# The six level products of two recurrences, split into 64-column halves of the TensorE array

## The chip, the core and the metric

The kernel runs on one core of one Trainium2 chip, in one launch. The time is device microseconds of that core, from one execution to the next; three runs of the kernel before are at hand, and one further execution that was profiled. TensorE (PE) does matrix products: a weight load puts the stationary operand into its 128 x 128 array (rows: what is summed over; columns: positions of the result), and a matmul streams the moving operand through it into PSUM. PE in a profile is its matmuls, PEld its weight loads. DVE is VectorE, ACT ScalarE.

## The reference, cut to what matters

The model is one first block of two layers and one second block. Two of its mixers are gated recurrences computed in chunks of 64 tokens, four heads each. Within a chunk they need a lower triangular matrix of weighted products (HGRN2 in the first block, GLA in the second; the two differ in head width, 128 and 64):

```python
b = jnp.cumsum(gi, axis=2)                                  # log decay in a chunk of 64
diff = b[:, :, :, None, :] - b[:, :, None, :, :]
dec = jnp.exp(jnp.where(tri, diff, -jnp.inf))
att = jnp.einsum('bhtk,bhtsk,bhsk->bhts', qi, dec, ki)      # t, s in one chunk
o_intra = jnp.einsum('bhts,bhsv->bhtv', att, vi)
```

Around them stand projections from 1024 columns, attention of two kinds, a pooling mixer, two MLPs, and a mixture of 32 experts.

## The kernel before, in words

The sequence has 512 tokens and 16 leading ones. Every float32 weight is split into a high and a low part and multiplied in three products (`dense`, L289), with loads of 512 KB streamed from memory; this is most of TensorE's work.

The decay in `att` depends on both positions and on the key, so it can't be taken out of the product at once. The kernel does it by levels: for w = 1, 2, 4, 8, 16, 32 (`LEVELS`), pairs of neighbouring blocks of w positions, the second against the first, get their decay relative to the block border. `level` (L518 to L540, DVE and ACT) makes one array x for a level, in which the first blocks hold the keys and the second blocks the queries; one matmul per tile of 128 tokens (two chunks) then multiplies x with itself. In `att_level` the stationary operand is the tile's 128 positions of x, the moving one the 64 positions that `second` picks (the second block of each pair), and the result stands in a PSUM tile of 128 x 64 (L557). A `copy_predicated` on DVE (L561) then takes the entries of that level by a mask (`self.msk`) into `at` (HGRN2) or `gat` (GLA). `att_diag` (L569) makes the diagonal before.

- `hgrn_head` runs four times, once a head: rows is one slice of 128, so a level is 4 matmuls, one a tile. For levels 0 to 3 a further small matmul does the 16 leading tokens (L767, 8 moving columns; L769 reads its first 16 rows).
- `gla_heads` runs twice, for two heads each: a pair of heads shares the 128 rows, 64 each, so a level is 8 matmuls, two a tile, one on array rows 0 to 63 and one on rows 64 to 127.

All of these products are plain float32. The trace has two weight loads and two matmul records for each such matmul in the program.

The kernel is written as generators (`weave`, `WEAVES`), which interleave a head of a recurrence with projections and attention; a scheduler then fixes the order on each engine when the program is built. So a level's matmuls stand as a group on TensorE between groups of L289 and of attention (L1020, L1034, L2053, L2060, L2035).

Of the kernel before, what the change touches and what calls it, by code (L numbers as in the profile page):

```python
# [20 lines left out]
NM = 16  # L21
# [179 lines left out]
class Ker:  # L201
# [347 lines left out]
    def att_level(self, i, x, rows, off, ats):  # L549

        nc = self.nc
        w = LEVELS[i]
        pas = [self.psb() for _ in rows]
        for j in range(NT):
            for pa, r in zip(pas, rows):
                xs = x[r, off + j * 128:off + (j + 1) * 128]
                nc.tensor.matmul(pa[:, j * 64:(j + 1) * 64], xs, self.second(xs, i), start=True, stop=True)  # L557
        nb = 64 // w
        m = self.msk[:, i, :].rearrange("p (n b) -> p n b", b=w)[:, None].to_broadcast([128, 4, nb, w])
        for pa, at in zip(pas, ats):  # L560
            nc.vector.copy_predicated(self.second(at, i), m, pa[:, :256].rearrange("p (j n b) -> p j n b", j=4, b=w))  # L561
# [174 lines left out]
    def hgrn_head(self, p1, hd, st):  # L736
        nc = self.nc
        kk, b, c, q, v = (st[n] for n in ("kk", "b", "c", "q", "v"))

        ks = self.tmp()  # L740
        e3 = ks[:, NM:].rearrange("p (c n) -> p c n", n=64)
        c3 = c[:, NM:].rearrange("p (c n) -> p c n", n=64)
        b3 = b[:, NM:].rearrange("p (c n) -> p c n", n=64)
        nc.vector.tensor_add(e3, c3, b3[:, :, 63:64].to_broadcast([128, 8, 64]))
        nc.vector.tensor_scalar(ks[:, :NM], c[:, :NM], b[:, NM - 1:NM], None, op0=OP.add)
        nc.scalar.activation(ks, ks, AF.Exp)
        dec = p1.tile([128, 8], F32, name="dec", bufs=2)
        nc.scalar.activation(dec, b3[:, :, 63], AF.Exp)

        at = p1.tile([128, 4, 128], F32, name="at")  # L750
        am = p1.tile([128, NM], F32, name="am")
        al = [slice(0, 128)]
        self.att_diag(kk, q, al, NM, [at])
        pa = self.psb()
        nc.tensor.matmul(pa[:, :NM], kk[:, :128], q[:, :NM], start=True, stop=True)
        nc.vector.tensor_mul(am, pa[:, :NM], self.ident[:, :NM])
        x = self.level(0, b, c, None, q, T, NM)
        yield
        kt = p1.tile([128, 5, 128], F32, name="kt")
        self.to_tokens(ks, kt)  # L760
        for i in range(6):
            nxt = self.level(i + 1, b, c, None, q, T, NM) if i < 5 else None
            yield
            self.att_level(i, x, al, NM, [at])
            if i < 4:
                pa = self.psb()
                nc.tensor.matmul(pa[:, :8], x[:, :128], self.second(x[:, :NM], i), start=True, stop=True)  # L767
                w = LEVELS[i]
                nc.vector.copy_predicated(self.second(am[:NM], i), self.msk[:NM, i, :8].rearrange("p (n b) -> p n b", b=w),  # L769
                                          pa[:NM, :8].rearrange("p (n b) -> p n b", b=w))  # L770
            x = nxt
        qp = self.tmp()
        nc.scalar.activation(qp, b, AF.Exp)
        nc.vector.tensor_mul(qp, qp, q)
        yield

        ps = [self.psb() for _ in range(2)]
        new = [ps[ch % 2][:, ch // 2 * 128:(ch // 2 + 1) * 128] for ch in range(8)]
        nc.tensor.matmul(new[0], kt[:, 4, :], v[:, 4, :], start=True, stop=True, skip_group_check=True)
        for ch in range(1, 8):  # L780
            j, par = divmod(ch - 1, 2)
            r = slice(par * 64, par * 64 + 64)
            nc.tensor.matmul(new[ch], kt[r, j, :], v[r, j, :], start=True, stop=True, skip_group_check=True)
        sts = []
        for ch in range(8):
            s1 = p1.tile([128, 128], F32, name="st", bufs=8)
            if ch == 0:
                nc.vector.tensor_copy(s1, new[ch])
            else:
                nc.vector.scalar_tensor_tensor(s1, sts[-1], dec[:, ch - 1:ch], new[ch], op0=OP.mult, op1=OP.add)  # L790
            sts.append(s1)
            if ch % 2:
                yield
        yield
        po = self.psb()
        for ch in range(8):
            j, par = divmod(ch, 2)
            if par == 0:
                nc.tensor.matmul(po[:, j * 128:(j + 1) * 128], v[:, j, :], at[:, j, :], start=True, stop=False,
                                 skip_group_check=True)  # L800
            nc.tensor.matmul(po[:, ch * 64:(ch + 1) * 64], sts[ch], qp[:, NM + ch * 64:NM + (ch + 1) * 64], start=False,
                             stop=par == 1, skip_group_check=True)
        pom = self.psb()
        nc.tensor.matmul(pom[:, :NM], v[:, 4, :], am, start=True, stop=True)
        o = self.tmp()
        nc.scalar.copy(o[:, NM:], po)
        nc.scalar.copy(o[:, :NM], pom[:, :NM])

        sq = self.tmp()
        nc.scalar.activation(sq, o, AF.Square)  # L810
        yield
        yield
        pn = self.ones_sum([(self.ones, sq)])
        ro = self.tmp()
        self.rstd_rows(self.v2(ro), pn, 128)
        while "g" not in st:
            yield
        g = st["g"]
        nc.vector.scalar_tensor_tensor(g, o, self.vec("hgain"), g, op0=OP.mult, op1=OP.mult)
        nc.vector.tensor_mul(self.o[hd], g, ro)  # L820
        yield
# [1298 lines left out]
```

## Time and profile before

| | |
|---|---|
| time, median of 3 runs | 1751.21 us (1749.43 to 1753.71) |
| the profiled execution | 1755.02 us, span 1753.1 us |
| PE busy | 1705.3 us, 97% of the span |
| PEld busy | 1497.2 us, 85% |
| DVE busy | 1090.5 us, 62% |
| ACT busy | 861.0 us, 49% |
| matmul records of L557 | 384, from 80.2 to 268.3 us and from 1255.6 to 1369.3 us |

Busy time is the union of the instructions' durations. A matmul's record lasts longer than its place in the stream, since successive matmuls overlap; what one costs in a row of them is read from the distance of the starts, or from the chain that ended last, where pieces stand end to end.

### The profile page before, as it was taken

What the parts mean: (1) busy time and instruction counts of PE and PEld (TensorE: products, weight loads), DVE (VectorE), ACT (ScalarE), POOL (GpSimd) and SP (SyncE); (2) the same over time, 40 slices, a digit from 0 to 9 for tenths busy, and PEclk for the clock granted to TensorE, in tenths of its full rate; (3) what the DMA queues carried; (4) which work ended last, traced back from release to release, by engine and by line L of the source; (5) the groups of instructions that cost most, each with busy time, mean ns of one, the idle gap of its engine ahead of it and who ended that gap; (6) DMA issues with size and microseconds to landing.
All of it is one profiled execution on the core that took longest, in us unless ns stands there. A gap on an engine that the chain in (4) does not pass through costs nothing.

```text
span 1753.1 us, 26914 instructions
## 1 busy us (share of the span) xinstructions
PE 1705.3 (97%) x10674; PEld 1497.2 (85%) x10674; DVE 1090.5 (62%) x1885; ACT 861.0 (49%) x1419; POOL 59.1 (3%) x65
## 2 busy tenths in 40 slices
PE   8999999999999999999999999999999999999996
PEld 8999999999999999878888888767767788888884
DVE  7678675633434344553434345589857768999995
ACT  6455654432323134441314144454346359999995
POOL 0000000000000000000000000100000000101102
PEclk9999999999999999999999999999969999999998
DMA  5211113232323222133333234322201458999993
GB/s 189 72 49 49 37 37 105 86 96 85 96 86 96 86 96 74 59 96 97 96 95 92 90 96 143 114 61 72 73 13 55 172 213 299 323 341 358 354 363 89
DMA packets 72339, 223.72 MB, mean 128 GB/s; under 512 B 9464, under 2 KB 9520, under 8 KB 72208
## 3 DMA queue, kind: packets, MB, share of 16 engines
q1 hardware_dynamic: 68976, 215.70, 36.7%
q0 software_dynamic: 3232, 6.25, 1.9%
q8 instruction: 85, 1.39, 0.3%
q14 instruction: 46, 0.38, 0.1%
HBM read 213.50 MB, written 12.60 MB: 129 GB/s over the span
## 4 chain that ended last, share of the span: by engine, by line
PE 91%; DVE 5%; ACT 2%; DMA 1%; issue 1%; SPq 0%; POOL 0%; POOLq 0%; DVEq 0%
PE pm L289 32%; PE ps L289 29%; PE ps L1589 6%; PE ps L1569 3%; PE ps L266 3%; PE ps L267 2%; PE ps L268 2%; PE ps L557 2%; DVE wlo L260 1%; PE ps L2060 1%; PE ps L2035 1%; PE ps L2053 1%; PE pm L485 1%; PE ps L1192 1%; DVE acc L1835 1%
## 5 line engine op out<-in xcount | busy, mean ns | idle before, releaser
L259 ACT CAST whi<-wraw 128x1024 fp32r<-128x1024 f32 (+1 forms) x309 | 321.3, 1045 | 606.1 <-PE pm L289 293.0
L260 DVE TENSOR_TENSOR wlo<-wraw,whi 128x1024 fp32r<-128x1024 f32 (+1 forms) x309 | 373.1, 1216 | 40.9 <-ACT whi L259 30.6
L289 PE MATMUL pm<-xh,whi 128*128 128x264 f32 x976 | 202.1, 288 | 8.4 <-ACT whi L259 6.0
L289 PE MATMUL pm<-xh,wlo 128*128 128x264 f32 x976 | 200.7, 286 | 0.5 <-DVE wlo L260 0.5
L289 PE MATMUL pm<-xl,whi 128*128 128x264 f32 x976 | 200.4, 287 | 0.1
L289 PE MATMUL ps<-xh,whi 128*128 128x512 f32 x472 | 191.8, 407 | 0.0
L289 PE MATMUL ps<-xh,wlo 128*128 128x512 f32 x472 | 186.1, 395 | 0.0
L289 PE MATMUL ps<-xl,whi 128*128 128x512 f32 x472 | 185.3, 393 | 0.0
L289 PEld LDWEIGHTS pm<-xh,whi 128*128 128x128 f32 x976 | 152.7, 190 | 9.4 <-ACT whi L259 6.0
L289 PEld LDWEIGHTS pm<-xh,wlo 128*128 128x128 f32 x976 | 152.4, 189 | 0.8 <-DVE wlo L260 0.7
L289 PEld LDWEIGHTS pm<-xl,whi 128*128 128x128 f32 x976 | 152.0, 189 | 0.7 <-DVE xl L467 0.6
L289 PEld LDWEIGHTS ps<-xh,whi 128*128 128x128 f32 x472 | 89.1, 189 | 23.5 <-issue 1.8
L289 PEld LDWEIGHTS ps<-xh,wlo 128*128 128x128 f32 x472 | 89.0, 189 | 21.0
L289 PEld LDWEIGHTS ps<-xl,whi 128*128 128x128 f32 x472 | 89.2, 189 | 19.5 <-issue 0.5
L1589 PE MATMUL ps<-wlo,xg 128*128 128x512 f32 x256 | 103.8, 405 | 1.3 <-DVE wlo L260 1.2
L289 PE MATMUL pm<-ah,whi 128*128 128x264 f32 x512 | 104.1, 284 | 0.0
L289 PE MATMUL pm<-ah,wlo 128*128 128x264 f32 x512 | 104.0, 285 | 0.0
L289 PE MATMUL pm<-al,whi 128*128 128x264 f32 x512 | 103.7, 284 | 0.0
L1589 PE MATMUL ps<-whi,xg 128*128 128x512 f32 x256 | 103.6, 405 | 0.0
L289 PE MATMUL ps<-ah,whi 128*128 128x512 f32 x256 | 101.1, 395 | 0.0
L289 PE MATMUL ps<-ah,wlo 128*128 128x512 f32 x256 | 101.0, 394 | 0.0
L289 PE MATMUL ps<-al,whi 128*128 128x512 f32 x256 | 100.5, 392 | 0.0
(500 smaller groups left out, 3216.1 us busy)
## 6 DMA issues: line engine op xcount, KB each, us to landing
wraw<-in_stream_dram SPq DMA_DIRECT2D x306, 512.0 KB, 3.7
t<-in_stream_dram SPq DMA_DIRECT2D x90, 256.0 KB, 6.9
h<-in_stream_dram SPq DMA_DIRECT2D x37, 512.0 KB, 5.9
h<-in_xT_dram SPq DMA_DIRECT2D x16, 264.0 KB, 3.3
hd<-h SPq DMA_DIRECT2D x8, 256.0 KB, 2.0
h<-hd SPq DMA_DIRECT2D x8, 256.0 KB, 3.3
out_dram<-t SPq DMA_DIRECT2D x8, 256.0 KB, 2.1
gt<-rbd POOLq DMA_DIRECT2D x4, 256.0 KB, 5.7
```

The costliest lines, as they stand in the source:

```text
L259: self.nc.scalar.copy(hi, src)
L260: i = self.nc.vector.tensor_sub(lo, src, hi.bitcast(F32))
L266: nc.tensor.matmul(ps, wh, xh, start=start, stop=False)
L267: nc.tensor.matmul(ps, wh, xl, start=False, stop=False)
L268: nc.tensor.matmul(ps, wl, xh, start=False, stop=stop)
L289: nc.tensor.matmul(ps, w[:, b, :], x[:, sl], start=(first and f and i == 0), stop=(last and l and i == nb - 1))
L485: nc.tensor.matmul(pm[:, s, :H2], l, r[:, s * H2:(s + 1) * H2], start=i == 0, stop=i == len(pairs) - 1)
L557: nc.tensor.matmul(pa[:, j * 64:(j + 1) * 64], xs, self.second(xs, i), start=True, stop=True)
L1192: nc.tensor.matmul(ps[:, i * 128:i * 128 + n], self.z[:, i, cols], self.bands[i][:, g, :n], start=False, stop=i == NT - 1, skip_group_chec ...
L1569: nc.tensor.matmul(pg[:, j * m:(j + 1) * m], src[2 * i + k // 4][:, sl], oh[:, i, :m], start=i == 0, stop=i == NT - 1, skip_group_check=True)
L1589: nc.tensor.matmul(pa, xk, v[:, k], start=kk == 0 and n == 0, stop=kk == 7 and n == 1, skip_group_check=True)
L1835: nc.vector.match_replace(out=acc, in_to_replace=m8, in_values=acc, imm_value=sel)
```

## The change

In `att_level` each matmul becomes two. The stationary operand is one chunk's 64 positions instead of the tile's 128; the result of chunk c goes to partitions 64c to 64c + 63 of the same PSUM tile, so chunk 0 uses array columns 0 to 63 and chunk 1 columns 64 to 127. The moving operand is the same 64 positions for both. What is in PSUM afterwards is the same. The small matmul for the leading tokens has 64 stationary columns too, on columns 0 to 63. No DVE or ACT instruction is changed, and no DMA. Lines behind it move down by 2 or 3.

```diff
         pas = [self.psb() for _ in rows]
+
         for j in range(NT):
-            for pa, r in zip(pas, rows):
-                xs = x[r, off + j * 128:off + (j + 1) * 128]
-                nc.tensor.matmul(pa[:, j * 64:(j + 1) * 64], xs, self.second(xs, i), start=True, stop=True)
+            for c in range(2):
+                for pa, r in zip(pas, rows):
+                    xs = x[r, off + j * 128:off + (j + 1) * 128]
+                    nc.tensor.matmul(pa[c * 64:(c + 1) * 64, j * 64:(j + 1) * 64], xs[:, c * 64:(c + 1) * 64], self.second(xs, i),
+                                     start=True, stop=True)
...
-                nc.tensor.matmul(pa[:, :8], x[:, :128], self.second(x[:, :NM], i), start=True, stop=True)
+                nc.tensor.matmul(pa[:64, :8], x[:, :64], self.second(x[:, :NM], i), start=True, stop=True)
```

The first place is TensorE in HGRN2's first head, at its third level; t is the array x of the level. Before:

```order
L289 MATMUL pm<-xh,whi 128x264 x2
L289 MATMUL pm<-xl,whi 128x264 x2
L289 MATMUL pm<-xh,wlo 128x264
L557 MATMUL ps<-t 128x64 x4
L767 MATMUL ps<-t 128x8
L289 MATMUL pm<-xh,wlo 128x264
```

and with the change:

```order
L289 MATMUL pm<-xh,whi 128x264 x2
L289 MATMUL pm<-xl,whi 128x264
L559 MATMUL ps<-t 64x64 x8
L770 MATMUL ps<-t 64x8
L289 MATMUL pm<-xl,whi 128x264
```

Four matmuls with 128 result rows have become eight with 64, chunk 0 and chunk 1 of a tile in turn, and the group stands two matmuls of the projection earlier.

The second place is TensorE in GLA's first pair of heads, between attention (L2060, L2053) and a projection; gt is x. Before:

```order
L2060 MATMUL ps<-va,t 128x64 x2
L2053 MATMUL ps<-c_97,t 128x128 x2
L557 MATMUL ps<-gt 128x64 x8
L289 MATMUL ps<-xh,whi 128x512
L289 MATMUL ps<-xl,whi 128x512
```

and with the change:

```order
L2063 MATMUL ps<-va,t 128x64 x2
L2056 MATMUL ps<-c_97,t 128x128 x2
L559 MATMUL ps<-gt 64x64 x16
L289 MATMUL ps<-xh,whi 128x512
L289 MATMUL ps<-xl,whi 128x512
```

Eight have become sixteen: for a tile rows 0 to 63 and 64 to 127 of chunk 0, then the same of chunk 1. The neighbours stand as before.

## Rows read from the trace of the kernel before

**Rows 1.** The page: engines' busy time, and the chain that ended last.

```profile
PE 1705.3 (97%) x10674; PEld 1497.2 (85%) x10674; DVE 1090.5 (62%) x1885; ACT 861.0 (49%) x1419; POOL 59.1 (3%) x65
PE 91%; DVE 5%; ACT 2%; DMA 1%; issue 1%; SPq 0%; POOL 0%; POOLq 0%; DVEq 0%
```

**Rows 2.** Windows: length, busy us of PE, PEld, DVE, ACT, POOL; granted clock, DMA.

```profile
80.00:100.00 20.00, 20.00 (x172) 20.00 (x170) 18.62 (x40) 10.37 (x18) 0.00 (x0) 1.00 0.26 79
...
1280.00:1285.00 5.00, 5.00 (x24) 3.29 (x23) 1.43 (x6) 0.30 (x2) 0.00 (x0) 0.50 0.39 108
...
1300.00:1310.00 10.00, 10.00 (x53) 7.21 (x51) 5.69 (x20) 3.90 (x13) 0.00 (x0) 0.72 0.01 2
...
1353.00:1370.00 17.00, 14.34 (x124) 11.64 (x123) 15.43 (x37) 6.49 (x9) 0.00 (x0) 0.90 0.20 64
```

**Rows 3.** Line 557: records, durations in ns, first and last start.

```profile
L557 PE MATMUL ps<-t x192: 217/275/303, 80.2 to 268.3; 128*128 128x64 f32 x192
L557 PE MATMUL ps<-gt x192: 268/272/473, 1255.6 to 1369.3; 64*128 64x64 f32 x192
```

**Rows 4.** The chain, 75 to 275 us: shares by line.

```profile
by line: PE pm L289 42.5%; PE ps L557 10.2%; PE ps L1034 4.3%; PE pm L1011 4.2%; PE pm L1012 3.8%; PE pm L485 2.8%; PE ps L801 2.4%; PE ps L1020 2.3%; PE ps L783 2.3%; PE ps L926 2.1%; PE ps L1032 1.8%; PE ps L799 1.6%; PE ps L509 1.6%; PE 
```

**Rows 5.** The chain, 264 to 271 and 1386 to 1390 us: start, length, line, records.

```profile
265.95 0.89 PE ps L1034 x8
266.85 1.73 PE ps L557 x16
...
1387.12 1.72 PE ps L489 x4
```

**Rows 6.** The chain, 1250 to 1400 us: pieces of L557.

```profile
1255.66 1.04 PE ps L557 x16
...
1270.41 1.09 PE ps L557 x16
...
1281.20 1.68 PE ps L557 x13
...
1367.67 1.93 PE ps L557 x32
```

**Rows 7.** Weight loads by form (stationary rows*columns): busy us, mean ns | idle before.

```profile
L557 PEld LDWEIGHTS ps<-t 128*128 128x128 f32 x192 | 23.3, 192 | 0.0
L266 PEld LDWEIGHTS ps<-whi,xh 128*16 128x16 f32 x8 | 0.8, 96 | 0.1
```

**Rows 8.** Timeline of PE, 78 to 82 us: start, length, line, records.

```profile
80.18 1.00 PE L557 MATMUL ps<-t 128*128 128x64 f32 x8
81.02 0.34 PE L767 MATMUL ps<-t 128*128 128x8 f32 x2
81.21 0.49 PE L289 MATMUL pm<-xh,whi 128*128 128x264 f32 x2
```

**Rows 9.** Timeline of PE, 1353.25 to 1353.35 us.

```profile
1353.30 0.33 PE L557 MATMUL ps<-gt 64*128 64x64 f32 x2
```

**Rows 10.** Timeline of PE, 1353 to 1356 us.

```profile
1352.98 0.40 PE L289 MATMUL ps<-xh,wlo 128*128 128x512 f32 x1
1353.30 2.00 PE L557 MATMUL ps<-gt 64*128 64x64 f32 x32
1355.24 0.50 PE L289 MATMUL ps<-xh,whi 128*128 128x512 f32 x1
1355.57 0.39 PE L289 MATMUL ps<-xl,whi 128*128 128x512 f32 x1
1355.80 0.40 PE L289 MATMUL ps<-xh,wlo 128*128 128x512 f32 x1
```

**Rows 11.** Timeline of PE, 682.4 to 684 us.

```profile
682.80 0.28 PE L268 MATMUL ps<-whi,xl 128*128 128x256 f32 x1
682.92 0.28 PE L266 MATMUL ps<-whi,xh 128*16 128x256 f32 x1
683.04 0.28 PE L267 MATMUL ps<-wlo,xh 128*16 128x256 f32 x1
```

## The prediction

> **What bounds the kernel now.** I read the page first. TensorE is busy for 97% of the span and carries 91% of the chain that ended last [rows 1]; no DMA and no other engine comes near. So time taken off TensorE comes off the span, unless the stretch has another engine close behind. Next come the lines of the change. L557 leaves 384 matmul records, two for each matmul in the program: 192 in HGRN2 (24 groups of 8, one a level and head) and 192 in GLA (12 groups of 16) [rows 3].
>
> Are these groups on the path? In HGRN2 they are: over the 200 us from 75 to 275 the chain gives L557 10.2%, 20.4 us [rows 4], and 24 groups at the 0.84 us of [rows 8] (first start of L557 to first start of L767) make 20.2. In GLA only some are: the chain names the groups from 1255.66 to 1270.41 (four), 13 of the 16 records of one at 1281.20, one more, and the two in the 32 records at 1367.67, so 8 of 12 [rows 6]. The others end before DVE does; from 1353 to 1370 DVE is busy for 15.43 of 17 us and TensorE for 14.34 [rows 2]. What they save is lost, and I count it as nothing.
>
> **What one record costs now.** Back to back, 16 records of HGRN2 take 1.73 us, 0.108 each [rows 5]. Two things could set that: the load of 128 stationary columns or the stream of 64 moving ones. L1034 streams 128 moving columns behind loads of 128 and takes 0.89 for 8, 0.111 each [rows 5]: twice the stream, the same step. So the load sets it. The stream alone is seen at L489, 512 columns: 1.72 for 4, 0.43 each [rows 5], hence 0.054 for 64, an estimate in proportion. How a load depends on its columns: a record of 128 columns lasts 192 ns, one of 16 columns 96 ns [rows 7]; 96 ns for 112 columns are 0.86 ns a column, so 64 columns take 0.055 us off the place that a load holds, about half. In GLA two records start together, one on each half of the rows: a window of 0.1 us holds both [rows 9]. There 32 records take 1.94 us [rows 10], 16 steps of 0.121 with the edges; inside I take 0.112, the bare step of [rows 5] with a little for the second start.
>
> **The change, part by part.**
> 1. *Twice as many records, each with half the load and the same stream.* If the halves of the columns work side by side, as the halves of the rows do now, a tile's two chunks make one step, of the larger of 0.055 (load) and 0.054 (stream); I take 0.060, the same few ns over the bare figure that 0.111 shows over twice 0.054. No row shows two column halves at work, so the step is bounded: 0.055 below, and above 0.120, two of these in turn, one for each chunk. I take the lower side, because the row halves do just this in the same kernel [rows 9].
> 2. *HGRN2.* The start of the first step hangs on the load before it, so 7 steps of a group change: 7 x (0.108 - 0.060) = 0.34 us, times 24 = 8.1 us.
> 3. *The small matmul L767.* Its two records hold 0.19 us until L289 goes on [rows 8]; with 64 columns between that and two steps of 0.060: nothing to 0.07. I take half, 0.035 x 16 = 0.5 us (it is there for four levels of four heads).
> 4. *GLA.* Four records share a step: 7 x (0.112 - 0.060) = 0.36, times 8 groups on the path = 2.9 us. The group at 1281.20 runs at half clock (1.68 us for 13 records against 1.04 for 16; the granted clock is 0.50 there [rows 2, 6]), which doubles its share: 0.3 more.
> 5. *DVE behind HGRN2's first head.* From 80 to 100 us DVE is busy for 18.62 of 20 [rows 2]. Six groups there save 2.1 us of TensorE, which leaves 17.9; DVE then sets the end of that stretch, and 0.7 is lost.
> 6. *The moves of the scheduler.* A group stands up to two L289 matmuls earlier or later; these have the same operands and lengths, and all of them are waited for later than that. Priced at 0, with 2 us either way in the range.
> 7. *DVE's reads (L561)* stay as they are; they may begin 0.3 us earlier, and nothing waits for them on the path in HGRN2.
>
> Sum: 8.1 + 0.5 + 2.9 + 0.3 - 0.7 = 11.1 us. The profiled execution took 1755.0, so 1743.9; the median of the runs stands 3.8 below it, which gives 1740.
>
> **A rule that speaks against it.** A group of GLA, which cuts the rows in half, pays for the change of shape: from the last L289 to its first record 0.32 us instead of the 0.23 of a step of L289; 1.94 us for 16 steps, 0.15 over 16 x 0.112; and the first L289 behind it takes 0.33 to the next instead of 0.23 [rows 10]. That is 0.34 us in and out. A stationary operand of 16 columns on all rows pays nothing: 682.80, 682.92 and 683.04 stand 0.12 apart, across the change of form and behind it [rows 11]. By these rows 64 columns cost HGRN2 nothing extra. The Trainium skill, "TensorEngine Tiling (Array Packing)", Key Properties, says that a change of tiling mode, not only of the tile, drains the engine. For cuts of the rows the trace agrees; for the cut of the columns the row shows none, but at the first columns alone. By the rule the sum would be worse by 22 x 0.34 = 7.5 us (22 places, since four of the 24 groups stand in pairs); that is the second rival.
>
> **The rivals.**
> - *The halves take turns* (the change doesn't do what it says): the loads are shorter, but the second half begins when the first is through. HGRN2: 15 steps of 0.060 against 7 of 0.108, +0.14 x 24 = 3.4; L767 -0.5; GLA, whose row halves still go together, 15 x 0.060 against 7 x 0.112, +0.12 x 8 = 0.9. Together +3.8: 1755. For it: both halves get their moving operand from the same rows. Against it: only that the row halves don't take turns.
> - *The cut of the columns drains TensorE:* each of 22 places pays the 0.34 us that GLA's groups pay [rows 10], so 7.5 us of the 11.1 are given back, 1748; together with turns 1762. Against it [rows 11].
> - *The load is not hidden* (the slower side): the second chunk's load waits for the first chunk's stream on the same rows, so each record costs load plus stream, 0.055 + 0.054, again about 0.111. HGRN2: 15 x 0.111 against 7 x 0.108, +0.91 x 24 = 21.8; GLA +0.90 x 8 = 7.2: 1780. It decides as soon as a record costs more than 0.050 in HGRN2 on average (7 x 0.108 over 15). Against it: L1034's loads lie behind the stream of the same rows today [rows 5]. The Trainium skill, "TensorE: Matmul & The Clock Gate", Part 3, says that a load overlaps a running matmul only where the row group differs (or into the spare weights); the trace shows that overlap on the same rows.
> - *TensorE can't take in records that fast.* The fastest run is 32 in 1.94 us, 0.060 each [rows 10]; no row shows a faster one. If that were its limit, HGRN2 would come out as with turns (+3.4), GLA at 31 x 0.060 against 7 x 0.112, +1.08 x 8 = 8.6; with L767 +11.5: 1763. Against it: two records start inside 0.1 us [rows 9].
>
> **How the numbers follow.** Side by side 0.50, 1740, its own range 1731 to 1747. Turns 0.20, no change to tell. Drain 0.12: alone 0.08 (1748, within 0.3%), with turns 0.04 (slower). Load not hidden 0.10, slower. Record rate 0.08, slower. Three runs of this kernel spread over 4.3 us, so about 0.3%, 5 us, can be told from none: faster 0.50, same 0.28, slower 0.22. One thing stands across all cases: TensorE's clock, which is granted at half (1.2 of 2.4 GHz) from about 1280 and until between 1300 and 1310 [rows 2], some 26 us that cost 13. A quarter of that more or less is 3.3 us. The lower end, 1731, is 1740 less these 3.3, 2.0 for the moves, 1.1 for a step of 0.055, 0.7 for DVE and 1.4 for GLA's other four groups. The own range ends at 1747, with the clock and the moves against it and a step of 0.070 (+2.3). The whole range ends at 1764, which takes in all but the unhidden load.
>
> **What would show it.** Right: L559 in HGRN2 with 16 records in about 0.5 us, L289 following without a gap; in GLA 32 records in about 0.65. Turns: 0.95 us for 16 records. Drain: over 0.3 us between L289 and L559 and again behind. Unhidden: 1.7 us. Rate: 1.9 us for GLA's 32. The prediction is wrong in its first part if the 16 records take longer than 0.84, and wrong in its sum if they don't and the time still doesn't fall: then DVE or the clock has it.

## The result, and the profile after

The change takes 1738.7 us in the median (1738.3 to 1739.4, 4 runs), the kernel before 1752.5 beside it (1749.4 to 1754.4): 0.9928 of the time, 95% interval 0.9910 to 0.9946, 13.8 us less in the medians and some 12.6 by the ratio. The forecast was 1740, 11 less. The time agrees; two of the terms behind it do not, and this is what the sections below are about. The profiled execution took 1738.3 us, its span 1736.5, 16.6 less than the span before.

The page of the changed kernel: busy times, and the chain.

```profile
PE 1687.3 (97%) x11058; PEld 1477.3 (85%) x11058; DVE 1090.9 (63%) x1885; ACT 860.9 (50%) x1419; POOL 59.2 (3%) x65
PE 90%; DVE 5%; ACT 2%; DMA 1%; issue 1%; SPq 0%; POOL 0%; DVEq 0%; POOLq 0%; ACTq 0%
```

TensorE is the bound as in [rows 1], with 384 matmul records more and 18 us of busy time less.

Line 559, matmul records and weight loads by form, which answer to [rows 3, 7]:

```profile
L559 PE MATMUL ps<-t x384: 218/222/274, 80.8 to 263.5; 128*64 128x64 f32 x192
L559 PE MATMUL ps<-gt x384: 215/218/366, 1251.4 to 1352.3; 64*64 64x64 f32 x192
...
L559 PEld LDWEIGHTS ps<-t 128*64 128x64 f32 x384 | 13.1, 137 | 3.4 <-issue 1.5 <-ACT t L1028 0.2 <-DVE mx L989 0.2
```

A load of 64 columns lasts 137 ns, of 128 it was 192: 0.055 us less, as worked out.

The timeline of TensorE in HGRN2's first head:

```profile
96.33 0.40 PE L289 MATMUL pm<-xh,wlo 128*128 128x264 f32 x2
96.66 0.69 PE L559 MATMUL ps<-t 128*64 128x64 f32 x16
97.27 0.51 PE L289 MATMUL pm<-lh,whi 128*128 128x264 f32 x2
97.62 0.40 PE L289 MATMUL pm<-ll,whi 128*128 128x264 f32 x2
```

Sixteen records stand within 0.61 us, from 96.66 to the next start at 97.27; in turns they would have taken about 0.95. So the two halves do work side by side. The same level in the kernel before:

```profile
96.65 0.41 PE L289 MATMUL pm<-xh,wlo 128*128 128x264 f32 x2
96.90 1.00 PE L557 MATMUL ps<-t 128*128 128x64 f32 x8
97.71 0.49 PE L289 MATMUL pm<-lh,whi 128*128 128x264 f32 x2
98.03 0.41 PE L289 MATMUL pm<-ll,whi 128*128 128x264 f32 x2
```

The edge ahead is new: the pair of L289 there holds 0.33 instead of 0.25. The pair behind holds 0.35, but it held 0.32 before already. The group itself takes 0.61 for 0.81. So 0.09 us are left at this level, where 0.34 was forecast.

The first level, which has the small matmul (L770) behind its group:

```profile
80.49 0.40 PE L289 MATMUL pm<-xh,wlo 128*128 128x264 f32 x2
80.83 0.69 PE L559 MATMUL ps<-t 128*64 128x64 f32 x16
81.34 0.23 PE L770 MATMUL ps<-t 128*64 128x8 f32 x2
81.50 0.51 PE L289 MATMUL pm<-xh,whi 128*128 128x264 f32 x2
```

Group and small matmul take 0.67 instead of the 1.03 of [rows 8], 0.16 of it the small matmul instead of 0.19. With the same edges some 0.25 are left, where 0.37 was forecast.

And in GLA, the two levels of the second pair of heads that answer to [rows 10]:

```profile
1337.14 0.40 PE L289 MATMUL ps<-xh,wlo 128*128 128x512 f32 x1
1337.46 1.18 PE L559 MATMUL ps<-gt 64*64 64x64 f32 x64
1338.57 0.50 PE L289 MATMUL ps<-xh,whi 128*128 128x512 f32 x1
1338.91 0.40 PE L289 MATMUL ps<-xl,whi 128*128 128x512 f32 x1
```

64 records take 1.11 us where 32 took 1.94, and the edges are what they were (0.32 ahead, 0.34 behind).

Where did 16.6 us come from? The chain of waits gives the same places in both kernels: the end of HGRN2's level products (L786), and L559 in GLA.

```profile
264.55 1.09 PE ps L786 x14
...
1251.44 0.63 PE ps L559 x32
...
1275.34 1.06 PE ps L559 x30
...
1351.38 1.09 PE ps L559 x64
```

L786 is L783 of before, which came at 269.25 in the chain there:

```profile
269.25 1.08 PE ps L783 x14
```

So the kernel is 4.7 us ahead when HGRN2 is done; the first group had started 0.65 later than before (80.83 against [rows 8]), so the stretch of HGRN2 gave 5.3. Not all of this is the groups'. Before, TensorE waited once for DVE between the first head and the second:

```profile
PE pm L876 <- DVE t L911: 1.1, 1, 1.1
```

In the change this wait is gone, which leaves about 4.2 for the groups. It is gone in HGRN2 alone and in the order by chunks (below) too, and stands at 1.1 us in every kernel that has HGRN2's level products as before; with HGRN2 in quarters (1.6) and with two levels at a time (1.1) it is back. The groups' places in the order may be the reason; no run tests this.

At the first group of GLA it is 4.2 ahead (1251.44 against 1255.66), at the group at half clock 5.9 (1275.34 against 1281.20), and at the last 16.3 (1351.38 against 1367.67) [rows 6]. So 10.4 of the 16.6 come between 1275 and 1351, where L559 itself can have saved little over 1. The windows of the change there:

```profile
1270.00:1275.00 5.00, 2.92 (x12) 2.07 (x12) 4.60 (x19) 3.62 (x11) 0.00 (x0) 0.61 0.01 3
1275.00:1280.00 5.00, 5.00 (x53) 3.43 (x53) 2.47 (x8) 0.13 (x1) 0.00 (x0) 0.71 0.36 105
1280.00:1285.00 5.00, 5.00 (x38) 3.63 (x37) 3.93 (x13) 2.72 (x7) 0.00 (x0) 1.00 0.00 0
```

The granted clock (the figure behind the busy times) falls to half at about 1271 and is full again before 1280, some 7 us; before it was at half from about 1278 into the window of 1300 to 1310 [rows 2], some 27. Twenty us less at half clock are the 10 us. The prediction had this as 3.3 either way.

### The profile page after: what moved, and what is told of

It reads as the page before. It is cut to its first block, busy times and chain, and to the rows that moved or that the text cites. A ratio compares the mean times of both kernels' runs of the same rounds, so it can differ in the third digit from the quotient of the medians.

```text
span 1736.5 us, 27684 instructions
## 1 busy us (share of the span) xinstructions
PE 1687.3 (97%) x11058; PEld 1477.3 (85%) x11058; DVE 1090.9 (63%) x1885; ACT 860.9 (50%) x1419; POOL 59.2 (3%) x65
## 4 chain that ended last, share of the span: by engine, by line
PE 90%; DVE 5%; ACT 2%; DMA 1%; issue 1%; SPq 0%; POOL 0%; DVEq 0%; POOLq 0%; ACTq 0%
PE pm L289 32%; PE ps L289 29%; PE ps L1592 6%; PE ps L1572 3%; PE ps L266 2%; PE ps L267 2%; PE ps L268 2%; DVE wlo L260 1%; PE ps L559 1%; PE ps L2063 1%; DMA wraw<-in_stream_dram 1%; ACT whi L259 1%; PE ps L2038 1%; PE ps L1195 1%; PE pm L485 1%
## 5 line engine op out<-in xcount | busy, mean ns | idle before, releaser
L289 PE MATMUL pm<-xh,whi 128*128 128x264 f32 x976 | 202.8, 289 | 8.9 <-ACT whi L259 6.0
L289 PE MATMUL pm<-xh,wlo 128*128 128x264 f32 x976 | 200.8, 287 | 0.0
L289 PE MATMUL pm<-xl,whi 128*128 128x264 f32 x976 | 200.8, 287 | 0.0
L289 PE MATMUL ps<-xh,whi 128*128 128x512 f32 x472 | 191.7, 406 | 0.0
L289 PE MATMUL ps<-xh,wlo 128*128 128x512 f32 x472 | 185.8, 394 | 0.0
L289 PE MATMUL ps<-xl,whi 128*128 128x512 f32 x472 | 185.4, 393 | 0.0
L289 PEld LDWEIGHTS pm<-xh,whi 128*128 128x128 f32 x976 | 153.1, 190 | 10.4 <-ACT whi L259 6.0
L289 PEld LDWEIGHTS pm<-xh,wlo 128*128 128x128 f32 x976 | 152.9, 190 | 0.0
L289 PEld LDWEIGHTS pm<-xl,whi 128*128 128x128 f32 x976 | 152.3, 190 | 0.6 <-DVE xl L467 0.3
L289 PEld LDWEIGHTS ps<-xh,whi 128*128 128x128 f32 x472 | 89.0, 189 | 23.7 <-issue 1.5
L289 PEld LDWEIGHTS ps<-xh,wlo 128*128 128x128 f32 x472 | 89.0, 188 | 20.9
L289 PEld LDWEIGHTS ps<-xl,whi 128*128 128x128 f32 x472 | 89.0, 189 | 19.3 <-issue 0.5
L289 PE MATMUL pm<-ah,whi 128*128 128x264 f32 x512 | 104.2, 284 | 0.0
L289 PE MATMUL pm<-ah,wlo 128*128 128x264 f32 x512 | 104.0, 285 | 0.0
L289 PE MATMUL pm<-al,whi 128*128 128x264 f32 x512 | 103.7, 284 | 0.0
L289 PE MATMUL ps<-ah,whi 128*128 128x512 f32 x256 | 101.1, 395 | 0.0
L289 PE MATMUL ps<-ah,wlo 128*128 128x512 f32 x256 | 101.0, 394 | 0.0
L289 PE MATMUL ps<-al,whi 128*128 128x512 f32 x256 | 100.5, 392 | 0.0
```

The source lines that it names most:

```text
L289: nc.tensor.matmul(ps, w[:, b, :], x[:, sl], start=(first and f and i == 0), stop=(last and l and i == nb - 1))
```

## The experiments

Theory A was the prediction's: the split costs nothing at its edges, and HGRN2 carries the gain. Theory B, made from the trace above: the halves go side by side, the change of the array's shape costs HGRN2 0.2 to 0.3 us a place, and the clock gave the rest. All times are beside runs of the kernel before on the same chip.

**HGRN2 alone.**

The edit is shown against the change; the other branch has the 128 columns of before.

```diff
-            for c in range(2):
+            for c in range(2 if len(rows) == 1 else 1):
...
```

> The halves in HGRN2 alone; GLA's level products as before. Theory A (the prediction's terms): the split costs nothing at its edges and HGRN2 carries most of the gain, about 8 us less than before, 1744. Theory B (from the trace of the change): the halves go side by side, but each of the 22 places pays about 0.2 to 0.3 us for the change of the array's shape, so HGRN2 gives 4 us, 1748, and most of the gain seen came from a shorter stretch at half clock around GLA. B expects the half-clock stretch behind 1270 us to be as long as before, about 27 us, unless the mere shift of 4 us changes it; then it is the moment that counts and not GLA's products.

1747.9 us against 1751.7; ratio 0.9970 (0.9958 to 0.9983). In its profile the clock is at half just as long as before:

```profile
1280.00:1290.00 10.00, 10.00 (x45) 8.58 (x46) 4.86 (x16) 3.00 (x7) 0.00 (x0) 0.50 0.00 0
1290.00:1300.00 10.00, 10.00 (x40) 7.01 (x38) 5.04 (x15) 2.70 (x6) 0.00 (x0) 0.50 0.01 2
```

HGRN2 gives 4 to 5 us (some 6 with the clock of before, since its six runs had 0.983 to 0.985), well under what A asked for, and an earlier arrival by itself doesn't shorten the stretch.

**GLA alone**, again shown against the change.

```diff
-            for c in range(2):
+            for c in range(2 if len(rows) == 2 else 1):
...
+                nc.tensor.matmul(pa[:, :8], x[:, :128], self.second(x[:, :NM], i), start=True, stop=True)
```

> The halves in GLA alone; HGRN2's level products and the small matmul as before. Theory A: 3 us less than before, 1749. Theory B: GLA's groups give 1.5 to 2 us by themselves, and if they also shorten the half-clock stretch from 27 to about 7 us, 10 more: 1740. If the stretch is as long as before, 1750, and then the clock hung on the moment of arrival.

1744.0 us against 1751.7; ratio 0.9948 (0.9934 to 0.9961), more than HGRN2. The clock is full from within the first ten us on:

```profile
1280.00:1290.00 10.00, 10.00 (x84) 7.32 (x85) 5.76 (x19) 3.43 (x10) 0.00 (x0) 0.77 0.14 54
1290.00:1300.00 10.00, 9.50 (x67) 6.70 (x64) 8.68 (x27) 4.98 (x15) 0.00 (x0) 1.00 0.00 0
```

B's picture holds: with GLA's halves the stretch is short. Its 1740 was 4 us too low.

**Chunk by chunk.** The same matmuls in another order: all tiles of chunk 0, then all of chunk 1.

```diff
-        for j in range(NT):
-            for c in range(2):
+        for c in range(2):
+            for j in range(NT):
```

> As the change, but all four tiles of chunk 0 first and then all of chunk 1 (the loop over chunks is the outer one). If each column half has a queue of its own, as the row parts seem to, the halves still go side by side and nothing changes: HGRN2 16 records in 0.5 us, 1739. If only neighbours in the program overlap, HGRN2's 16 records take about 0.95, 24 x 0.45 = 10 us more, 1749.

1750.1 us, ratio 0.9995 (0.9983 to 1.0008): the gain is gone. The timeline of its TensorE:

```profile
97.05 0.97 PE L559 MATMUL ps<-t 128*64 128x64 f32 x16
97.95 0.51 PE L289 MATMUL pm<-lh,whi 128*128 128x264 f32 x2
```

Sixteen records take 0.90 us instead of 0.61. Only neighbours in the program overlap; the change works because its inner loop puts the halves next to each other. This is also the nearest thing to the rival of turns, and it shows its price. The clock of its ten runs, 0.984 to 0.988, is that of the kernel before, although GLA is cut in halves here too.

**The small matmul alone**, at 64 columns, with the level products of before.

```diff
-                nc.tensor.matmul(pa[:, :8], x[:, :128], self.second(x[:, :NM], i), start=True, stop=True)
+                nc.tensor.matmul(pa[:64, :8], x[:, :64], self.second(x[:, :NM], i), start=True, stop=True)
```

> The kernel before, with one part of the change alone: the small matmul behind HGRN2's levels 0 to 3 has 64 stationary columns, at the first columns of the array; all level products as before. If it is the second half of the columns (or two halves at work) that makes TensorE drain, nothing is paid and the pieces are as before or shorter: 1750 to 1752. If any stationary operand of 64 columns drains it, each of the 16 places pays 0.2 to 0.3 us: the step from L557 to the small matmul about 0.2 instead of 0.11, L289 behind it again 0.2, and 3 to 4 us more, 1755.

1754.3 us against 1751.4; ratio 1.0013 (1.0000 to 1.0025). Its timeline, beside [rows 8]:

```profile
80.28 1.00 PE L557 MATMUL ps<-t 128*128 128x64 f32 x8
81.22 0.28 PE L767 MATMUL ps<-t 128*64 128x8 f32 x2
81.43 0.51 PE L289 MATMUL pm<-xh,whi 128*128 128x264 f32 x2
```

From the first L557 to L767 it is 0.94 instead of 0.84. So a stationary operand of 64 columns costs 0.10 us at the change of shape, at the first columns alone and with nothing beside it. The small matmul then holds 0.21 instead of 0.19.

**The small matmul at 16 columns.**

```diff
+                nc.tensor.matmul(pa[:NM, :8], x[:, :NM], self.second(x[:, :NM], i), start=True, stop=True)
```

> The kernel before with the small matmul of HGRN2 at 16 stationary columns (all that it needs), the level products as before. With 64 columns at the same place TensorE paid 0.13 us a place, although a 16-column operand elsewhere (in the low and high parts, not plain float32) paid nothing. If any narrower cut of the columns drains it in plain float32, the same 0.1 us or more stands between L557 and the small matmul: 1753 to 1754. If 16 columns are exempt, the step is as before or shorter, and the time 1750 to 1751 (16 x 0.07 less at most).

1752.9 us against 1753.2; ratio 0.9998 (0.9988 to 1.0008).

```profile
80.58 1.00 PE L557 MATMUL ps<-t 128*128 128x64 f32 x8
81.51 0.21 PE L767 MATMUL ps<-t 128*16 128x8 f32 x2
81.65 0.51 PE L289 MATMUL pm<-xh,whi 128*128 128x264 f32 x2
```

The same 0.93; only the matmul itself is shorter (0.14 to L289). So 16 columns aren't exempt either. What sets [rows 11] apart, where 16 columns paid nothing, is not the width; those are the high and low parts, not plain float32, with 256 moving columns. Which of these it is was not tried.

**Quarters everywhere**: 32 stationary columns, the 32 moving positions of the own chunk, and two copies of half the size on DVE.

```diff
-            for c in range(2):
+            for q in range(4):
...
+                    nc.tensor.matmul(pa[q * 32:(q + 1) * 32, j * 32:(j + 1) * 32], xs[:, q * 32:(q + 1) * 32],
+                                     self.second(xs[:, q // 2 * 64:(q // 2 + 1) * 64], i), start=True, stop=True)
...
+            for c in range(2):
+                h = slice(c * 64, (c + 1) * 64)
...
+                nc.vector.copy_predicated(self.second(at[h, :, h], i), m, pa[h, :128].rearrange("p (j n b) -> p j n b", j=4, b=w))
```

> Both recurrences: 32 stationary columns a matmul (four column tiles at once), and only the 32 moving positions of their own chunk; DVE reads the two chunks with two copies of half the size. If a step is the larger of load and stream, both are halved against the change, 0.030 us a step: HGRN2 32 records in 0.25 to 0.3 instead of 0.5, 24 x 0.23 = 5.5 us less than the change, GLA 1.5 to 2 less: 1731 or so. If TensorE takes in no more than a record in 0.017 us (the change shows 64 records of GLA in 1.09 us), HGRN2's 32 take 0.54 and GLA's 64 take 1.09, no gain: 1738 or a little over, with DVE's extra copies.

1740.0 us, ratio 0.9928 (0.9914 to 0.9941): no better than the change. On TensorE the two recurrences answer differently:

```profile
95.93 0.46 PE L559 MATMUL ps<-t 128*32 128x32 f32 x32
96.32 0.51 PE L289 MATMUL pm<-lh,whi 128*128 128x264 f32 x2
...
1248.10 0.76 PE L559 MATMUL ps<-gt 64*32 64x32 f32 x64
1248.79 0.50 PE L289 MATMUL ps<-xh,whi 128*128 128x512 f32 x1
```

HGRN2's group falls to 0.39 us, as halved loads and streams have it. GLA's stays at 0.69 (0.63 in the change): 64 records, 0.011 each on average. The pace is not even, as the window from 1248.00 to 1248.30 shows:

```profile
1248.10 0.36 PE L559 MATMUL ps<-gt 64*32 64x32 f32 x32
```

Half of the 64 have started within 0.20 us, and the other half take the rest. What holds them back is not shown.

**Quarters in HGRN2 only**, with the small matmul at 32 columns and GLA as in the change.

> GLA as the change. HGRN2 in quarters: 32 stationary columns a matmul, the 32 moving positions of the own chunk, two copies of half the size on DVE; the small matmul has 32 stationary columns too, so that no further change of shape stands between it and the group. The run with quarters everywhere had HGRN2's groups at 0.39 us instead of 0.62, so 24 x 0.23 = 5.4 us less than the change if TensorE sets the pace: 1733. If the 0.2 us at each edge, DVE (near its limit from 80 to 100 us) or the clock take it, 1737 to 1739.

1737.5 us, ratio 0.9933 (0.9910 to 0.9957); one of its six runs stood at 1747.9 with a mean clock of 0.982. The 5.4 us of TensorE don't arrive. The window of HGRN2's first head, and a line of its timeline:

```profile
80.00:100.00 20.00, 18.96 (x293) 17.61 (x294) 19.65 (x46) 11.61 (x20) 0.00 (x0) 1.00 0.23 81
...
88.88 0.43 PE L561 MATMUL ps<-t 128*32 128x32 f32 x29 [0.52 <-DVE t L539]
```

DVE is busy for 19.65 of the 20 us (18.62 before [rows 2]), and TensorE now waits for it. The busy share alone doesn't tell this, for the change has 19.64 in the same window and no wait:

```profile
80.00:100.00 20.00, 20.00 (x228) 18.80 (x227) 19.64 (x41) 11.37 (x20) 0.00 (x0) 1.00 0.27 80
```

From 75 to 275 us the waits of TensorE come to 5.0 us, to 2.2 in the change. Behind the longest the clock falls, to 0.96 in the mean of 100 to 145 us, which takes 1.8 us more (1.00 in the change):

```profile
PE pm L891 <- DVE t L926: 1.6, 1, 1.6
...
100.00:145.00 45.00, 43.25 (x300) 39.47 (x299) 30.46 (x65) 27.60 (x49) 2.44 (x6) 0.96 0.18 58
```

Together these are 4.6 of the 5.4.

**Two levels at a time**, to change the shape less often.

```diff
+                for g, xx in ((i, x), (i + 1, y)):
+                    self.att_level(g, xx, al, NM, [at])
```

> The change, with HGRN2's levels issued two at a time, so that the array's shape changes less often: in the program's order 11 places or so fewer have a change on both sides or stand with a projection between. Each place saved is worth 0.2 to 0.3 us on TensorE: 1 to 3 us less than the change, 1736 to 1738, if the later start of the first of each pair makes nobody wait; 1739 or more if it does.

1739.0 us, ratio 0.9927 (0.9913 to 0.9940): nothing gained over the change. The scheduler put other work between many of the pairs: in its trace the cut matmuls of HGRN2 stand at 21 separate places, in that of the change at 26, so 5 were saved and not 11. And the later start makes TensorE wait, 4.9 us from 75 to 275 instead of 2.2:

```profile
PE ps L1026 <- ACT t L997: 3.2, 5, 1.2
PE pm L882 <- DVE t L917: 1.1, 1, 1.1
```

**Which group of GLA holds the clock?** The halves in one group alone, and in all but that one.

```diff
+            self.att_level(i, x, rows, 0, ats, f == 0 and i == 5)
```

> The kernel before, with the halves only in one GLA group: the last level of the first pair of heads, which runs inside the stretch at half clock near 1281 us. If that group (long at half clock) holds the clock down, the stretch shortens from up to 27 to about 7 us in most runs: mean granted clock 0.988 and about 7 us less, 1745. If it is the groups in front of it, which let TensorE arrive earlier or wait longer, the clock stays at 0.983 to 0.987 and the time at 1751.

> The counterpart: the halves in all of GLA's groups but that one. If that group holds the clock down, clock 0.983 to 0.987 and 1749 (2 us from the other groups). If it is the groups in front, clock 0.988 and 1744, as with all of GLA.

Neither decides it. One group alone: 1749.8 us (1746.9 to 1753.1, 12 runs), ratio 0.9991 (0.9979 to 1.0002), clock 0.984 to 0.989. All but it: 1747.6 us, ratio 0.9994 (0.9975 to 1.0012), but eight runs from 1745.6 to 1748.7 and four from 1755.3 to 1760.2, clock 0.978 to 0.988. The profile of one of these four shows a stretch longer than ever:

```profile
1290.00:1300.00 10.00, 10.00 (x42) 7.31 (x40) 5.59 (x17) 1.65 (x4) 0.00 (x0) 0.50 0.01 2
1300.00:1310.00 10.00, 10.00 (x38) 7.02 (x36) 4.47 (x15) 3.33 (x11) 0.00 (x0) 0.50 0.00 0
```

**The change again.**

> The change itself again, beside more runs of the kernel before, for the granted clock of many executions. If all of GLA's groups together keep the half-clock stretch short, the clock is 0.987 or more in nearly all runs of the change and the times lie within 3 us; if it is chance, some runs show 0.982 to 0.986 and stand 5 to 10 us higher, as the kernel before does in about half of its runs.

1737.3 us (1737.0 to 1740.8, 6 runs) against 1753.2; ratio 0.9922 (0.9906 to 0.9937). The spread is 3.8 us, a little over the 3 expected. With the four runs of the result, the mean granted clock of the change is 0.988 to 0.990 in all ten. The kernel before had 0.982 to 0.988 in the 62 runs beside the experiments, mean 0.9856, and its times, 1747 to 1757, follow the clock. All kernels with the halves in the whole of GLA side by side (the change, GLA alone, both kinds of quarters, two levels at a time) had 0.987 or more in 31 of 32 runs.

## Why the prediction was right, and where it was not

Mean times: 1751.9 us for 62 runs of before, 1738.5 for ten of the change, 13.4 less. The time that the clock takes is (1 - granted clock) x span: 0.0144 x 1750 = 25.2 us before, 0.0111 x 1737 = 19.3 after. So about 6 us of the 13.4 are clock, and 7.4 are the change's own work. The runs of before bear this sum out: a line through the 62 gives 1.6 us for each 0.001 of clock, and the sum has 1.75. The prediction had 11.1 for the work and 0 for the clock.

1. *Side by side*: right. The step of 0.060 is 0.058, which is how far apart the pairs of records start in the trace from the second pair on; the load's 0.055 is 0.055. The order by chunks shows that it hangs on neighbours.
2. *HGRN2, 8.1 + 0.5 us*: the groups gave about 4.2. The step that failed is the one that priced the edges at nothing, "By these rows 64 columns cost HGRN2 nothing extra". At the level from 96.66 on, 0.34 us was forecast and 0.09 are left: 0.08 more go ahead of the group, 0.03 more in the pair behind, and the group saves 0.20, because its first pair of records holds 0.11 and its end 0.15. Where the small matmul stands behind a group some 0.25 are left. The small matmul by itself was sized right, 0.03. The rival's 7.5 us for 22 places was too high: the edges took 4.4 of the 8.6, for part of the exit that [rows 10] shows for GLA was paid before too (the pair behind held 0.32), and the small matmul has the shape of its group. The term 6, the moves, was priced at 0; the wait that is gone, 1.1 us, stands there, inside its 2 either way. One row of another data type [rows 11] was taken for this case; the small matmul at 64 and at 16 columns shows that plain float32 pays. The Trainium skill's rule in "TensorEngine Tiling (Array Packing)", Key Properties, that a change of tiling mode drains the engine, agrees with this: about 0.1 us is lost ahead of a group; [rows 11] stays an exception.
3. *GLA, 0.36 us a group*: right, 0.41 (1.04 to 0.63). By HGRN2's 5.3 its share of the 7.4 is 2.1; GLA alone gave 7.7 us, of which (0.988 against 0.9856 of the clock) about 4 are clock, so 3 to 4. The prediction had 3.2. The two halves of the change, each by itself and at one clock, give 6 and 3 to 4, which is some 2 more than both at once; the split between them is known no better than that. What the groups off the path save is lost, as forecast: from 1250 to 1400 us L557 waited 2.7 us for DVE's gt, and L559 waits 3.8.
4. *DVE in the first head*, 0.7 us lost: not paid. TensorE is busy for all of 80 to 100 us in the change. DVE is near its limit, and the quarters reached it.
5. *The clock*: named as what cuts across all cases, but sized at 3.3 us and left out of the sum. It gave 6. That all of GLA's halves shorten the stretch at half clock is shown by GLA alone and the repeated runs; HGRN2 alone doesn't. How they do it stays open: one group, or all the others, moved the clock in some runs and not in others. In chunk order, with GLA's halves in turn, the clock is as before, so the cut alone doesn't do it. What TensorE did ahead of the fall is much the same in both kernels: it waited twice for attention's softmax on ACT, 3.5 us for L2046 before and 3.6 for the same line (L2049) in the change.

So the time came out within 2 us of the forecast by luck. HGRN2's groups gave 4.4 less than forecast and GLA, by this account, 1.1 less; on the other side lay 6 us from the clock, not counted, 1.1 from a wait that went, and 0.7 that DVE didn't take.

The rivals: turns, an unhidden load and a record rate of 0.060 us are shown wrong for this change (0.61 us for 16 records, 0.63 for GLA's 32). Whether a lower record rate holds the quarters back is open. The drain is right in kind and smaller than priced.

## What to carry to other kernels

Narrow float32 stationary operands gained here when matmuls for different column halves stood next to each other in the program, since load and stream of the halves then overlapped; put the loop over halves innermost. Going from the full to the cut array cost some 0.1 us, and the end of a group up to 0.15, so the cut paid best where groups were long or the array was cut already, as in GLA. A total that agrees with the forecast proves none of its terms: compare the same place in both traces, and set the granted clock of many runs beside the times before a gain is put down to the work.

## What the runs showed of the hardware

- Four matmul parts, two halves of the rows by two of the columns, work at once: 64 records in 1.11 us, 0.017 each, where two at once gave 0.060.
- With quarters 64 records of GLA take 0.69 us, 0.011 each, and the first 32 start within 0.20; cutting further gained nothing there.
- Overlap needs neighbours: the same 16 records took 0.61 us in one order and 0.90 in the other.
- A small matmul of 64 or of 16 columns, in plain float32, started 0.10 or 0.09 us later behind matmuls of 128 columns than one of 128.
- The kernel before ran from 1747 to 1757 us with a mean granted clock from 0.988 down to 0.982. Over the kernels' traces the stretch at half clock behind the softmax waits lasted from some 7 us (the change) to over 30 (GLA's halves in all groups but one).
